# The layer norm's factor and offset of the token tiles, on GpSimd at the head of a sublayer or on VectorE among its later steps

## The chip, the cores and the metric

The kernel runs on one core of a Trainium2 chip. The metric is the time of one launch in microseconds (us) of the device. The engines are named as in the profile: PE is TensorE (PEld its weight loads), DVE is VectorE, ACT is ScalarE, POOL is GpSimd, SP is SyncE, whose queue issues nearly all loads.

## What is computed

Two networks of the same plan run behind each other in fp32 on 256 tokens of 1024 channels: six sublayers in all. Each takes the residual stream, modulates it, runs a mixer or an expert layer, and normalizes the weighted sum:

```python
for i in range(DEPTH):
    ...
    hx = modulate(xs, sh1, sc1)                  # h * (1 + scale) + shift
    ...                                          # a mixer gives yx
    xs = layer_norm(alpha * xs + g1 * yx, ln_g[i, 0], ln_b[i, 0])
    hx = modulate(xs, sh2, sc2)
    ...                                          # peer, or a second mixer, gives fx
    xs = layer_norm(alpha * xs + g2 * fx, ln_g[i, 1], ln_b[i, 1])
```

The layer norm ends in `(h - mu) * rsqrt(var + eps) * g + b`, where g and b are rows of 1024 numbers. The sublayers s = 0 to 5 are mixer_ab, peer, mixer_pool, peer, moba and gdn. peer is an expert layer: queries, scores against keys, two rounds of top 16, a gather of experts by one-hot products, and sums.

## The kernel before

**Tiles.** The stream of tokens is two tiles `xs[0]` and `xs[1]` of 128 tokens by 1024 channels. Every product in fp32 is three matmuls (`mm3`, L130 to L132) of operands that are split into a rounded part and a rest. For a weight tile of 128x1024 `split_w` makes the rounded part on ACT (L94) and the rest on DVE (L95, both inputs in SBUF). For activations `split_a` does the same in pieces of up to 512 columns (L124 on ACT, L125 on DVE). A weight comes by a 512 KB load into one of four `raw` buffers (SP queue, L87), and its two parts go into one of three buffers each.

**Head of a sublayer.** `restart(s)`, for s = 1 to 5, stands between the norm of the sublayer before and the first product. The norm leaves `xs` normalized, but without g and b (L322 and L324 the reciprocal root, L368 a column, L373 on ACT and L375 on DVE the tiles). PE transposes `xs` (L409), and ACT (L413) and DVE (L415, from PSUM) put g, b and the modulation into one affine step, which gives `hf`; `split_a` makes the pair `h` from it, and the first products of the sublayer read `h` piece by piece. The residual needs `xs` with g and b too, but not before the sublayer's end, where `mix` (L346 to L348) adds the result. For it GpSimd multiplies `xs` by the row of g and adds the row of b, from the tile `lngb` that is loaded in the head:

```python
self.tail = i0.ins, i1.ins
for t in range(NT):
    x = self.xs[t]
    nc.gpsimd.tensor_tensor(x, x, gb[:, 0], op=ALU.mult)      # L424
    nc.gpsimd.tensor_tensor(x, x, gb[:, 1], op=ALU.add)       # L425
```

These are four operations of 128x1024 in each head, twenty in all.

**What sets the order.** The framework's scheduler orders each engine's instructions by the dependences and its own model of time. `issue_after(i)` keeps an instruction behind i, and `keep_in_program_order` keeps the code's order. `tail` is the pair of the last affine steps of the head, and `held` makes the splits of the two weights behind the first one wait for `tail`.

**What follows the heads.** In peer (s = 1 and 3) 16 steps `hp` each make a query by a linear step of 24 matmuls of 256 columns, then scores (L756) and two top-16 searches on DVE (L964 to L968); in steps 4 and 5 `xs` is also kept in DRAM (L771) for the residual. mixer_pool (s = 2) starts with two halves `nb` of four steps with 512-column products, moba (s = 4) with four halves, between which `ada_cols` multiplies and sums tiles of a modulation matrix on DVE (L284). gdn (s = 5) begins with a loop over b of linear steps and convolutions, and a small product with `wab` for its gates (split on DVE in L1156).

**The end.** The last norm has g and b in it: `mix_end` gives ACT and GpSimd the columns from 704 (tile 0) or 832 (tile 1) on (L380 to L382), and DVE the columns before them (L385, L386). L387 stores the result.

Of the kernel before, what the change touches and what calls it, by code (L numbers as in the profile page):

```python
# [11 lines left out]
F32 = mybir.dt.float32  # L12
# [10 lines left out]
NT = 2  # L23
# [18 lines left out]
class Net:  # L42
    def __init__(self, ctx, tc, a):
# [73 lines left out]
    def split_a(self, pool, src, n, tag, x1=None, x2=None):  # L117
        nc = self.nc
        if x1 is None:
            x1 = pool.tile([P, n], F32R, tag=tag + "1", name=self.nm(tag))  # L120
            x2 = pool.tile([P, n], F32R, tag=tag + "2", name=self.nm(tag))
        for o in range(0, n, 512):
            s = slice(o, min(o + 512, n))
            nc.scalar.activation(x1[:, s], src[:, s], AF.Copy)  # L124
            nc.vector.tensor_tensor(x2[:, s], src[:, s], x1[:, s].bitcast(F32), op=ALU.subtract)  # L125
        return x1, x2
# [147 lines left out]
    def ada_cols(self, i, cb, row):  # L274
# [86 lines left out]
    def mix_end(self, t):  # L361
# [9 lines left out]
        if self.last is None:  # L371
# [5 lines left out]
        g, b = self.last[:, 0], self.last[:, 1]  # L377
        k = (704, 832)[t]
        c = slice(k, D)
        nc.scalar.activation(z[:, c], z[:, c], AF.Identity, bias=nmr, scale=r)  # L380
        nc.gpsimd.tensor_tensor(z[:, c], z[:, c], g[:, c], op=ALU.mult)
        nc.gpsimd.tensor_tensor(z[:, c], z[:, c], b[:, c], op=ALU.add)  # L382
        c = slice(0, k)
        self.tc.keep_in_program_order(
            nc.vector.scalar_tensor_tensor(z[:, c], z[:, c], mv[:, 0:1], g[:, c], op0=ALU.subtract, op1=ALU.mult))  # L385
        nc.vector.scalar_tensor_tensor(z[:, c], z[:, c], r, b[:, c], op0=ALU.mult, op1=ALU.add)  # L386
        nc.sync.dma_start(self.a["out"][t], z)  # L387
# [6 lines left out]
    def restart(self, s, pool, h=None):  # L394
# [16 lines left out]
        for q, pt in enumerate(pts):  # L411
            kc = q * 2
            i0 = nc.scalar.activation(hf[:, kc], pt[:, 0].rearrange("p t c -> p (t c)"), AF.Identity,  # L413
                                 bias=ab[:, 1, kc:kc + 1], scale=ab[:, 0, kc:kc + 1])
            i1 = nc.vector.tensor_scalar(hf[:, kc + 1], pt[:, 1].rearrange("p t c -> p (t c)"),  # L415
                                    ab[:, 0, kc + 1:kc + 2], ab[:, 1, kc + 1:kc + 2], op0=ALU.mult, op1=ALU.add)
            for k in ((kc, kc + 1), (kc + 1, kc + 2)) if q == 0 else ((kc, kc + 2),):
                k = slice(*k)
                self.split_a(None, *(z[:, k].rearrange("p k t -> p (k t)") for z in (hf,)), (k.stop - k.start) * T, "",
                             *(z[:, k].rearrange("p k t -> p (k t)") for z in h))  # L420
        self.tail = i0.ins, i1.ins
        for t in range(NT):
# [291 lines left out]
    def peer(self, li, s, pool):  # L714
# [28 lines left out]
        with tc.tile_pool(name=self.nm("tk"), bufs=1) as tk:  # L743
# [19 lines left out]
            for hp in range(16):  # L763
# [224 lines left out]
    def mixer_pool(self, h, pool):  # L988
# [38 lines left out]
    def moba(self, h, pool):  # L1027
# [98 lines left out]
    def gdn(self, h, hf, pool):  # L1126
# [537 lines left out]
```

## Time and profile before

| what | value |
|---|---|
| time, median of 3 runs | 2500.62 us (2500.24 to 2500.70) |
| the profiled execution, its own time | 2504.04 us |
| its span, first to last instruction | 2502.2 us |
| mean granted clock of PE | 0.986 of full |
| PE busy | 2410.9 us (96%) |
| DVE busy | 1864.3 us (75%) |
| ACT busy | 1195.4 us (48%) |
| POOL busy | 158.5 us (6%) |
| DMA | 210 GB/s over the span |

All times within the program are of the profiled execution, whose own time stands beside its span: 1.8 us lie around the span. A row of the timeline gives the start, the duration, the engine, the line, the operation and its operands, and in brackets how long the engine was idle before it and what released it. `x2` at the end of a timeline row means that two alike are merged, with their time together.

### The profile page before, as it was taken

The numbers are of one execution on the slowest core, as the hardware profiler recorded it, in microseconds if no ns is written. First come the engines' busy times: TensorE is split into PE (matmuls) and PEld (weight loads), VectorE is DVE, ScalarE is ACT, GpSimd is POOL, SyncE is SP. The second block draws the span as 40 slices with busy tenths as digits, with TensorE's granted clock in tenths as the row PEclk, the third lists the DMA queues.
The fourth block names the chain that finished last, engine by engine and source line by source line (L and its number), as shares of the span: only waits on it lengthen the run. The fifth ranks groups of instructions, "written<-read, shape, count | busy, mean of one in ns | idle before, by whom it ended". The sixth has DMA issues, their size and how long they took to land.

```text
span 2502.2 us, 41876 instructions
## 1 busy us (share of the span) xinstructions
PE 2410.9 (96%) x15572; PEld 2131.3 (85%) x15572; DVE 1864.3 (75%) x3825; ACT 1195.4 (48%) x1980; POOL 158.5 (6%) x126
## 2 busy tenths in 40 slices
PE   8999899999999999998999999999999998998997
PEld 5875799999998777887899999998778887897886
DVE  3446699767776788876699767776888767787866
ACT  3345444544445444454544544445444554446533
POOL 1111200000000000001100000000000001003431
PEclk9999999999999999999999999999999999998999
DMA  8436557765557888975456765557899876863312
GB/s 296 132 134 228 179 169 220 238 194 177 176 173 245 290 306 307 311 246 185 160 171 216 239 200 177 172 179 241 302 310 311 271 219 198 278 221 121 110 59 68
DMA packets 196557, 527.42 MB, mean 211 GB/s; under 512 B 22104, under 2 KB 84984, under 8 KB 195200
## 3 DMA queue, kind: packets, MB, share of 16 engines
q1 hardware_dynamic: 160128, 488.70, 60.2%
q10 hardware_dynamic: 36224, 36.04, 4.1%
q8 instruction: 122, 2.00, 0.3%
q14 instruction: 83, 0.68, 0.1%
HBM read 489.76 MB, written 34.90 MB: 210 GB/s over the span
## 4 chain that ended last, share of the span: by engine, by line
PE 65%; DVE 14%; DMA 4%; issue 3%; ACT 2%; POOL 1%; SPq 0%; POOLq 0%; DVEq 0%; ACTq 0%
PE mm L132 10%; PE mm L131 10%; PE mm L130 10%; PE acc L132 9%; PE acc L130 9%; PE acc L131 9%; PE acc L827 4%; DVE w L95 4%; DMA raw<-peer_v 2%; ACT w L94 1%; DVE tk L965 1%; PE mm L1345 1%; DVE h L125 1%; DVE idx L968 1%; DVE raw L284 1%
## 5 line engine op out<-in xcount | busy, mean ns | idle before, releaser
L94 ACT ACTIVATE w<-raw 128x1024 fp32r<-128x1024 f32 x686 | 725.5, 1058 | 942.2 <-PE mm L131 490.1
L95 DVE TENSOR_TENSOR w<-raw,w 128x1024 fp32r<-128x1024 f32 x686 | 847.7, 1237 | 352.2 <-ACT w L94 350.6
L130 PE MATMUL mm<-h,w 128*128 128x256 f32 x2624 | 762.0, 291 | 4.4 <-ACT w L94 2.5
L131 PE MATMUL mm<-h,w 128*128 128x256 f32 x2624 | 747.8, 285 | 13.1 <-DVE h L125 13.0
L132 PE MATMUL mm<-h,w 128*128 128x256 f32 x2624 | 749.8, 286 | 7.0 <-DVE w L95 6.8
L131 PEld LDWEIGHTS mm<-h,w 128*128 128x128 f32 x2624 | 507.2, 193 | 16.5 <-DVE h L125 15.4
L132 PEld LDWEIGHTS mm<-h,w 128*128 128x128 f32 x2624 | 506.2, 193 | 11.2 <-DVE w L95 11.0
L130 PEld LDWEIGHTS mm<-h,w 128*128 128x128 f32 x2624 | 507.4, 193 | 6.4 <-ACT w L94 2.9
L130 PE MATMUL acc<-w,x 128*128 128x512 f32 x1024 | 405.2, 396 | 2.3 <-ACT x L124 2.2
L132 PE MATMUL acc<-w,x 128*128 128x512 f32 x1024 | 402.6, 397 | 4.2 <-DVE x L125 4.0
L131 PE MATMUL acc<-w,x 128*128 128x512 f32 x1024 | 404.1, 395 | 0.0
L132 PEld LDWEIGHTS acc<-w,x 128*128 128x128 f32 x1024 | 192.2, 188 | 58.1 <-DVE x L125 13.4
L130 PEld LDWEIGHTS acc<-w,x 128*128 128x128 f32 x1024 | 192.7, 188 | 49.6 <-ACT x L124 5.4
L131 PEld LDWEIGHTS acc<-w,x 128*128 128x128 f32 x1024 | 192.5, 188 | 44.5
L816 DVE TENSOR_TENSOR hot<-cols,sel 128x512 f32<-128x512 f32 x128 | 88.6, 692 | 112.6 <-PE acc L827 112.6
L324 POOL TENSOR_TENSOR rs<-rv,mhalf 128x1 f32<-128x1 f32 (+2 forms) x38 | 31.8, 836 | 2152.8 <-DVE rv L322 2151.7
L124 ACT ACTIVATE x<-ga 128x256 fp32r<-128x256 f32 x256 | 104.3, 408 | 110.9 <-DVE ga L862 105.1
L820 DVE TENSOR_SCALAR hot<-cols,sel 128x128 f32<-128x128 f32 x512 | 142.2, 341 | 0.0
L827 PE MATMUL acc<-hot 128*128 128x128 f32 x1024 | 134.9, 274 | 0.0
L827 PEld LDWEIGHTS acc<-hot 128*128 128x128 f32 x1024 | 125.4, 192 | 0.0
L132 PE MATMUL acc<-w,h 128*128 128x512 f32 (+1 forms) x296 | 116.4, 395 | 8.5 <-DVE h L125 8.5
L130 PE MATMUL acc<-w,h 128*128 128x512 f32 (+1 forms) x296 | 116.9, 398 | 4.4 <-ACT h L124 4.3
(381 smaller groups left out, 2747.2 us busy)
## 6 DMA issues: line engine op xcount, KB each, us to landing
raw<-peer_u SPq DMA_DIRECT2D x256, 512.0 KB, 3.6
raw<-peer_v SPq DMA_DIRECT2D x256, 512.0 KB, 4.7
raw<-adaT SPq DMA_DIRECT2D x96, 512.0 KB, 4.5
spill<-ga ACTq DMA_DIRECT2D x242, 128.0 KB, 2.3
ga<-spill SPq DMA_DIRECT2D x242, 128.0 KB, 4.5
raw<-ada SPq DMA_DIRECT2D x48, 512.0 KB, 3.9
raw<-ab_w_in SPq DMA_DIRECT2D x32, 512.0 KB, 3.6
raw<-peer_wq SPq DMA_DIRECT2D x32, 512.0 KB, 3.5
```

What stands on the lines that cost most here:

```text
L94: nc.scalar.activation(w1, raw, AF.Copy)
L95: nc.vector.tensor_tensor(w2, raw, w1.bitcast(F32), op=ALU.subtract)
L124: nc.scalar.activation(x1[:, s], src[:, s], AF.Copy)
L125: nc.vector.tensor_tensor(x2[:, s], src[:, s], x1[:, s].bitcast(F32), op=ALU.subtract)
L130: mm(ps, l[0], r[0], start=start, stop=False)
L131: mm(ps, l[0], r[1], start=False, stop=False)
L132: mm(ps, l[1], r[0], start=False, stop=stop)
L284: nc.vector.scalar_tensor_tensor(rx, rx, 1.0, cb[x], op0=ALU.mult, op1=ALU.mult, accum_out=part[:, x, k:k + 1])
L324: nc.gpsimd.tensor_tensor(r, v, self.mhalf[:, :n], op=ALU.pow)
L816: nc.vector.tensor_tensor(hot[:, 0], iota[:, None].to_broadcast([P, G, P]), sel[:, 0, n0:n0 + G, None].to_broadcast([P, G, P]), op=ALU.is_ ...
L820: nc.vector.tensor_scalar(hot[:, 1, g], iota, sel[:, 1, n:n + 1], sel[:, 2, n:n + 1], op0=ALU.is_equal, op1=ALU.mult)
L827: nc.tensor.matmul(ps[:, g * P:(g + 1) * P], hot[:, 0, g], hot[:, 1, g], start=True, stop=True)
```

## The change

The operations L424 and L425 leave GpSimd. `restart` puts them on a list `todo`, and `later()` takes one of it and issues it on DVE behind `tail`. It is called once in each step `hp` from 2 on of peer, in each step of mixer_pool's second half, in each even step of moba's first two halves, and in each round b from 1 on of gdn's convolution loop; `mix_begin`, at the end of a sublayer, does what is left. With it go:

- `tail` is now the pair of the last split of `h`, so that the held weights and `ada_cols` (L284, now L287) stand behind it.
- peer keeps `xs` in DRAM in steps 6 and 7.
- The last norm is done by DVE alone, over all 1024 columns (L384, L385).
- A tile `X` of gdn has a place of its own in SBUF, where it shared one with `lngb`.

```diff
+        self.ends = i.ins, j.ins                      # split_a: its last pair
...
+                with self.tc.issue_after(self.tail[1]):
+                    nc.vector.scalar_tensor_tensor(rx, rx, 1.0, cb[x], op0=ALU.mult, op1=ALU.mult, accum_out=part[:, x, k:k + 1])
...
+        while self.todo:
+            self.later()
...
-        nc.gpsimd.tensor_tensor(z[:, c], z[:, c], g[:, c], op=ALU.mult)
-        nc.gpsimd.tensor_tensor(z[:, c], z[:, c], b[:, c], op=ALU.add)
...
+            nc.vector.scalar_tensor_tensor(z, z, mv[:, 0:1], g, op0=ALU.subtract, op1=ALU.mult))
+        nc.vector.scalar_tensor_tensor(z, z, r, b, op0=ALU.mult, op1=ALU.add)
...
-        self.tail = i0.ins, i1.ins
-        for t in range(NT):
-            x = self.xs[t]
-            nc.gpsimd.tensor_tensor(x, x, gb[:, 0], op=ALU.mult)
-            nc.gpsimd.tensor_tensor(x, x, gb[:, 1], op=ALU.add)
+        self.tail = self.ends
+        self.todo = [(self.xs[t], gb[:, x], (ALU.mult, ALU.add)[x]) for t in range(NT) for x in range(2)]
...
+    def later(self):
+        if self.todo:
+            x, y, op = self.todo.pop(0)
+            with self.tc.issue_after(self.tail[1]):
+                self.nc.vector.tensor_tensor(x, x, y, op=op)
...
-                if hp in (4, 5):
-                    tc.keep_in_program_order(nc.scalar.dma_start(kept[hp - 4], self.xs[hp - 4]))
+                if hp > 1:
+                    self.later()
+                if hp in (6, 7):
+                    tc.keep_in_program_order(nc.scalar.dma_start(kept[hp - 6], self.xs[hp - 6]))
...
-        X, XT = (pt_([P, NT * D], tg).rearrange("p (t h c) -> p t h c", t=NT, h=H) for tg in ("b1", "XT"))
+        X, XT = (pt_([P, NT * D], tg).rearrange("p (t h c) -> p t h c", t=NT, h=H) for tg in ("X", "XT"))
```

GpSimd has 24 instructions fewer (the twenty and four of the end), DVE 19 more, ACT 4 fewer. PE has as many as before, and on SP one load (the last norm's rows) stands 23 places earlier.

DVE, head of s = 1 (peer), from the first splits of `h` to the first top-16 search, before (a row's `out<-in` are the program's names with numbers; `w` is a weight's rest, `vals` a search):

```order
L125 TENSOR_TENSOR h_2376<-hf_2384,h_2375 128x256 x2
L415 TENSOR_SCALAR hf_2384<-mm_2389,ab_2380 128x256
L125 TENSOR_TENSOR h_2376<-hf_2384,h_2375 128x512
L415 TENSOR_SCALAR hf_2384<-mm_2390,ab_2380 128x256
L125 TENSOR_TENSOR h_2376<-hf_2384,h_2375 128x512
L95 TENSOR_TENSOR w_2463<-raw_2460,w_2462 128x1024
L125 TENSOR_TENSOR h_2376<-hf_2384,h_2375 128x512
L95 TENSOR_TENSOR w_2496<-raw_2493,w_2495 128x1024
L95 TENSOR_TENSOR w_2529<-raw_2526,w_2528 128x1024
L95 TENSOR_TENSOR w_2572<-raw_2569,w_2571 128x1024
L964 MAX vals_2455<-sc_2459 128x8
```

The same place after:

```order
L126 TENSOR_TENSOR h_2376<-hf_2384,h_2375 128x256 x2
L414 TENSOR_SCALAR hf_2384<-mm_2389,ab_2380 128x256
L126 TENSOR_TENSOR h_2376<-hf_2384,h_2375 128x512
L414 TENSOR_SCALAR hf_2384<-mm_2390,ab_2380 128x256
L126 TENSOR_TENSOR h_2376<-hf_2384,h_2375 128x512 x2
L429 TENSOR_TENSOR xs_96<-xs_96,lngb_2385 128x1024
L96 TENSOR_TENSOR w_2459<-raw_2456,w_2458 128x1024
L96 TENSOR_TENSOR w_2492<-raw_2489,w_2491 128x1024
L96 TENSOR_TENSOR w_2525<-raw_2522,w_2524 128x1024
L969 MAX vals_2451<-sc_2455 128x8
L969 MAX vals_2452<-sc_2455 128x8
```

The last split of `h` moved ahead of the weight's split, the first of the four moved operations (L429) stands between them, and the first search has three weight splits ahead of it where it had four; the other three L429 follow among the searches.

DVE, head of s = 4 (moba), from the norm's end on, before:

```order
L368 SCALAR_TENSOR_TENSOR nmr_22102<-mv_22096,rs_22100 128x1
L375 TENSOR_SCALAR xs_22038<-xs_22038,mv_22096,rs_22100 128x512
L284 SCALAR_TENSOR_TENSOR raw_22272,adap_22271<-raw_22272,cb_22238 128x512 x2
L415 TENSOR_SCALAR hf_22118<-mm_22123,ab_22112 128x256
L415 TENSOR_SCALAR hf_22118<-mm_22121,ab_22112 128x256
L415 TENSOR_SCALAR hf_22118<-mm_22122,ab_22112 128x256
L125 TENSOR_TENSOR h_22117<-hf_22118,h_22116 128x256 x2
```

The same place after:

```order
L380 TENSOR_SCALAR xs_22038<-xs_22038,mv_22096,rs_22100 128x512
L414 TENSOR_SCALAR hf_22118<-mm_22123,ab_22112 128x256
L414 TENSOR_SCALAR hf_22118<-mm_22124,ab_22112 128x256
L414 TENSOR_SCALAR hf_22118<-mm_22121,ab_22112 128x256
L414 TENSOR_SCALAR hf_22118<-mm_22122,ab_22112 128x256
L126 TENSOR_TENSOR h_22117<-hf_22118,h_22116 128x256
```

The two L284, which stood between the norm and the first affine step, have left this place; they come behind the head's splits.

DVE, the end of the program, before:

```order
L368 SCALAR_TENSOR_TENSOR nmr_26012<-mv_25970,rs_25974 128x1
L385 SCALAR_TENSOR_TENSOR xs_22037<-xs_22037,mv_25970,b_25808 128x704
L386 SCALAR_TENSOR_TENSOR xs_22037<-xs_22037,rs_25974,b_25808 128x704
L368 SCALAR_TENSOR_TENSOR nmr_26020<-mv_26006,rs_26010 128x1
L385 SCALAR_TENSOR_TENSOR xs_22038<-xs_22038,mv_26006,b_25808 128x832
L386 SCALAR_TENSOR_TENSOR xs_22038<-xs_22038,rs_26010,b_25808 128x832
```

After, the same six stand there with 1024 columns each in L384 and L385, and neither ACT nor GpSimd has a part in these tiles.

## Rows read from the trace of the kernel before

**Rows 1.** The page: busy time of the engines; shares of the chain

```profile
PE 2410.9 (96%) x15572; PEld 2131.3 (85%) x15572; DVE 1864.3 (75%) x3825; ACT 1195.4 (48%) x1980; POOL 158.5 (6%) x126
...
PE 65%; DVE 14%; DMA 4%; issue 3%; ACT 2%; POOL 1%; SPq 0%; POOLq 0%; DVEq 0%; ACTq 0%
```

**Rows 2.** Groups by line, GpSimd: shapes xcount | busy, mean ns | idle before

```profile
L425 POOL TENSOR_TENSOR xs<-xs,lngb 128x1024 f32<-128x1024 f32 x10 | 27.9, 2799 | 0.3
```

**Rows 3.** Timeline of the head of s = 1: DVE, GpSimd, then PE

```profile
293.04 0.53 DVE L415 TENSOR_SCALAR hf<-mm,ab 128x256 f32<-128x256 f32 x1
293.50 2.40 DVE L125 TENSOR_TENSOR h<-hf,h 128x512 fp32r<-128x512 f32 x1
...
298.60 3.38 DVE L95 TENSOR_TENSOR w<-raw,w 128x1024 fp32r<-128x1024 f32 x1
...
304.67 1.21 DVE L95 TENSOR_TENSOR w<-raw,w 128x1024 fp32r<-128x1024 f32 x1
...
311.23 0.48 DVE L964 MAX8 vals<-sc 128x8 f32<-128x128 f32 x2
...
292.68 5.45 POOL L424 TENSOR_TENSOR xs<-xs,lngb 128x1024 f32<-128x1024 f32 x2 [3.40 <-ACT h L124]
...
304.80 0.58 PE L131 MATMUL mm<-h,w 128*128 128x256 f32 x1 [1.33 <-DVE h L125]
...
308.91 0.61 PE L756 MATMUL mm<-keys,qT 128*128 128x128 f32 x4
```

**Rows 4.** Windows: length, busy (x) of PE PEld DVE ACT POOL, PEclk, DMA share, GB/s

```profile
350.00:430.00 80.00, 76.55 (x620) 74.66 (x619) 79.93 (x248) 37.46 (x60) 0.00 (x0) 1.00 0.67 195
...
1173.00:1178.00 5.00, 5.00 (x13) 3.81 (x13) 4.25 (x5) 1.06 (x1) 0.00 (x0) 0.50 0.32 110
1178.00:1225.00 47.00, 47.00 (x243) 40.68 (x242) 23.83 (x26) 26.85 (x38) 0.00 (x0) 1.00 0.61 203
...
2137.00:2175.00 38.00, 34.05 (x188) 29.11 (x187) 26.31 (x51) 14.79 (x18) 0.00 (x0) 0.96 0.83 288
...
2262.00:2275.00 13.00, 9.05 (x45) 7.28 (x46) 8.37 (x6) 1.79 (x3) 10.32 (x9) 0.54 0.34 117
2275.00:2315.00 40.00, 40.00 (x337) 37.21 (x336) 32.23 (x73) 35.14 (x83) 5.90 (x7) 1.00 0.37 119
```

**Rows 5.** Timeline of the head of s = 2: DVE, then PE

```profile
1165.15 8.69 DVE L125 TENSOR_TENSOR h<-hf,h 128x256 fp32r<-128x256 f32 x5
...
1172.70 0.79 PE L132 MATMUL acc<-w,h 128*128 128x512 f32 x1 [4.07 <-DVE h L125]
```

**Rows 6.** Timeline of the head of s = 3: DVE

```profile
1237.75 3.23 DVE L125 TENSOR_TENSOR h<-hf,h 128x256 fp32r<-128x256 f32 x2
...
1247.59 0.68 DVE L125 TENSOR_TENSOR h<-hf,h 128x512 fp32r<-128x512 f32 x1
```

**Rows 7.** Timeline of the head of s = 4: DVE, then PE

```profile
2100.87 2.29 DVE L368 SCALAR_TENSOR_TENSOR nmr<-mv,rs 128x1 f32<-128x1 f32 x1 [0.66 <-POOL rs L324]
...
2103.54 2.85 DVE L284 SCALAR_TENSOR_TENSOR raw<-raw,cb 128x512 f32<-128x512 f32 x1
...
2103.67 1.97 PE L409 MATMUL mm<-ident,xs 128*128 128x128 f32 x8 [3.27 <-DVE xs L375]
```

**Rows 8.** Timeline of the head of s = 5: DVE, then GpSimd

```profile
2258.46 1.74 DVE L95 TENSOR_TENSOR w<-raw,w 128x1024 fp32r<-128x1024 f32 x1 [1.63 <-ACT w L94]
...
2266.19 2.42 DVE L1156 TENSOR_TENSOR wab<-wab,wab 128x128 fp32r<-128x128 f32 x1
...
2256.75 5.65 POOL L424 TENSOR_TENSOR xs<-xs,lngb 128x1024 f32<-128x1024 f32 x2 [5.88 <-DMA lngb<-ln_rows]
```

**Rows 9.** Timeline of the program's end: DVE, then GpSimd

```profile
2491.51 0.95 DVE L385 SCALAR_TENSOR_TENSOR xs<-xs,mv,b 128x704 f32<-128x704 f32 x1
...
2494.10 1.07 DVE L385 SCALAR_TENSOR_TENSOR xs<-xs,mv,b 128x832 f32<-128x832 f32 x1
...
2497.30 0.59 POOL L382 TENSOR_TENSOR xs<-xs,b 128x192 f32<-128x192 f32 x1
```

More of the change, by code (lines that the diff above doesn't have):

```diff
@@ L68, in __init__ @@
         self.held = 0
+        self.todo = []
     def nm(self, s):
@@ L123, in split_a @@
             s = slice(o, min(o + 512, n))
-            nc.scalar.activation(x1[:, s], src[:, s], AF.Copy)
-            nc.vector.tensor_tensor(x2[:, s], src[:, s], x1[:, s].bitcast(F32), op=ALU.subtract)
+            i = nc.scalar.activation(x1[:, s], src[:, s], AF.Copy)
+            j = nc.vector.tensor_tensor(x2[:, s], src[:, s], x1[:, s].bitcast(F32), op=ALU.subtract)
+        self.ends = i.ins, j.ins
         return x1, x2
@@ L283, in ada_cols @@
                 rx = r[:, x * 512:(x + 1) * 512]
-                nc.vector.scalar_tensor_tensor(rx, rx, 1.0, cb[x], op0=ALU.mult, op1=ALU.mult, accum_out=part[:, x, k:k + 1])
+                with self.tc.issue_after(self.tail[1]):
+                    nc.vector.scalar_tensor_tensor(rx, rx, 1.0, cb[x], op0=ALU.mult, op1=ALU.mult, accum_out=part[:, x, k:k + 1])
             if k == KC - 1:
@@ L377, in mix_end @@
         g, b = self.last[:, 0], self.last[:, 1]
-        k = (704, 832)[t]
-        c = slice(k, D)
-        nc.scalar.activation(z[:, c], z[:, c], AF.Identity, bias=nmr, scale=r)
-        nc.gpsimd.tensor_tensor(z[:, c], z[:, c], g[:, c], op=ALU.mult)
-        nc.gpsimd.tensor_tensor(z[:, c], z[:, c], b[:, c], op=ALU.add)
-        c = slice(0, k)
         self.tc.keep_in_program_order(
-            nc.vector.scalar_tensor_tensor(z[:, c], z[:, c], mv[:, 0:1], g[:, c], op0=ALU.subtract, op1=ALU.mult))
-        nc.vector.scalar_tensor_tensor(z[:, c], z[:, c], r, b[:, c], op0=ALU.mult, op1=ALU.add)
+            nc.vector.scalar_tensor_tensor(z, z, mv[:, 0:1], g, op0=ALU.subtract, op1=ALU.mult))
+        nc.vector.scalar_tensor_tensor(z, z, r, b, op0=ALU.mult, op1=ALU.add)
         nc.sync.dma_start(self.a["out"][t], z)
@@ L412, in restart @@
             kc = q * 2
-            i0 = nc.scalar.activation(hf[:, kc], pt[:, 0].rearrange("p t c -> p (t c)"), AF.Identity,
+            nc.scalar.activation(hf[:, kc], pt[:, 0].rearrange("p t c -> p (t c)"), AF.Identity,
                                  bias=ab[:, 1, kc:kc + 1], scale=ab[:, 0, kc:kc + 1])
-            i1 = nc.vector.tensor_scalar(hf[:, kc + 1], pt[:, 1].rearrange("p t c -> p (t c)"),
+            nc.vector.tensor_scalar(hf[:, kc + 1], pt[:, 1].rearrange("p t c -> p (t c)"),
                                     ab[:, 0, kc + 1:kc + 2], ab[:, 1, kc + 1:kc + 2], op0=ALU.mult, op1=ALU.add)
@@ L995, in mixer_pool @@
         for nb in range(2):
-            for t, ps in enumerate(self.lin_nat(a["pool_w_in"][nb], 4, xa)):
+            pss = [self.acc() for _ in xa]
+            for _ in self.lin_steps(a["pool_w_in"][nb], 4, xa, pss):
+                if nb == 1:
+                    self.later()
+            for t, ps in enumerate(pss):
                 nc.scalar.copy(hin[:, t, nb * 512:nb * 512 + 512], ps)
@@ L1039, in moba @@
                     next(ada, None)
+                else:
+                    self.later()
             for t, ps in enumerate(pss):
@@ L1475, in gdn @@
             conv_mm(b)
+            if b:
+                self.later()
             next(ga, None)
```

## The prediction

> **What bounds the kernel now.** I read the page first. TensorE is busy for 96% of the span and has 65% of the chain that ended last; VectorE, busy for 75%, has another 14%, and GpSimd is busy for only 6% [rows 1]. So the bulk of the time is products, and the work that the change moves is small: GpSimd's additions (L425) take 27.9 us for ten and its multiplications about as much [rows 2], with nobody reading their result before the sublayer's end. By their own duration they cost nothing. The question is what else they do, and for that I read the timeline of each head, VectorE against GpSimd.
>
> There a pattern shows. In the head of s = 1 GpSimd's first pair starts at 292.68 and lasts 5.45 us, and the second pair (mean 2.80 us each [rows 2]) follows, so GpSimd works until about 304. In this stretch VectorE's split of 128x512 takes 2.40 us and its weight split 3.38 us; the next weight split, at 304.67, takes 1.21 us [rows 3]. In s = 3 the head's last split of 128x512 takes 0.68 us, where the first two of 128x256, as many columns together, take 3.23 [rows 6]. The affine step L415, whose input is in PSUM, takes 0.53 us in the middle of the slow stretch [rows 3]. So it is VectorE's operations with two inputs in SBUF that stretch to 2.4 to 3.5 times while GpSimd works on `xs`. TensorE waits for them (1.33 us before 304.80 [rows 3] is one of several such waits), and behind these waits its granted clock falls: 0.50 in the 5 us from 1173, 0.54 in the 13 us from 2262, where it is 1.00 in the long stretches behind [rows 4]. That is the lower of its two levels, 1.2 GHz against 2.4.
>
> The Trainium skill, page "SBUF — State Buffer", section "Who interferes with whom", has a rule for it: a VectorE instruction with two inputs in SBUF contends with a GpSimd instruction that reads SBUF, since its second input comes through the port that GpSimd uses; with one such input it does not. The rows agree (2.40 against 0.68 us, and 0.53 for the step from PSUM). By it the whole excess goes once GpSimd's reads are gone.
>
> **The change part by part.** I walk through each head with VectorE's durations from outside GpSimd's work: 0.68 us for 512 columns of split, 1.21 us for a weight split, 0.53 us for L415. The moved operation, 128x1024 with two inputs in SBUF, isn't in the trace on VectorE; the weight split has the same shape and operands, so I take 1.21 us for it. Twenty of them are 24.2 us of new VectorE work.
>
> *s = 1 (peer).* From 293.50 on three splits and one L415 stand ahead of the end of `h`: 3 x 0.68 + 0.53 gives 296.1, and I allow 0.6 us for ACT's rounded parts, which must come first (an estimate): 296.7, against 304.67. Then come the first L429 and the weight split that the second query waits for, to 299.1, and 22 matmuls at 0.123 us (76.55 us for 620 [rows 4]), to 301.8. Before, this point was 308.91 [rows 3]: TensorE is 7.1 us earlier. But VectorE, which does the top-16 searches from here on, is busy for 79.93 of the 80 us from 350, and TensorE already loses 3.45 us there [rows 4]. Its first search could start at 302.5 instead of 311.23, 8.7 us earlier, with three L429 and one weight split more behind it than before: 4.8 us of that are paid back, 3.9 stay. So the gain lies between 3.9 and 7.1; I take 4.7, near VectorE's end, as VectorE is the fuller of the two. If TensorE's clock falls in its new wait before 299.1, 22 matmuls take 2 to 3 us longer, and 2 is left.
>
> *s = 2 (mixer_pool).* Five splits, 2048 columns, take 8.69 us from 1165.15 [rows 5]; at 0.68 for 512 they take 2.7, so `h` ends 5.9 us earlier. TensorE's wait of 4.07 us for it [rows 5] goes with that, and so should the 5.0 us at clock 0.50 behind it, worth up to 2.5 more; I take 1.3 of it, since the weight splits follow close. 7.2, from 6 to 8.4. The four L429 fall in the second half, where VectorE is busy for 23.83 of 47 us [rows 4]: covered. Without that cover they would cost 4.8.
>
> *s = 3 (peer).* From 1237.75 to the last split's end at 1248.27 VectorE does 2048 columns of split, two L415 and one weight split [rows 6]: 10.5 us for 2.7 + 1.1 + 1.2 = 5.0. So 5.5 on TensorE's line; on VectorE's, three L429 (3.6) go off: 1.9. I take 3.2, from 1.5 to 5.5.
>
> *s = 4 (moba).* Two L284 of 2.85 us stand between the norm and the first L415, and L368, a single column, takes 2.29 us [rows 7]. The L284 go behind the head's splits, and L368 shrinks to that of a column: I count 2.0. TensorE's transposes, 1.97 us, ran beside the L284 [rows 7] and now stand on the path. 5.7 - 2.0 + 2.0 gives 5.7, and some 0.5 more comes from the splits that overlap GpSimd's end: 6.2 for the first products. What limits this gain stands behind it: from 2137 to 2175 the DMA engines are 83% busy at 288 GB/s, and TensorE is idle for 4 of 38 us [rows 4]. The loads start earlier only as buffers come free earlier. I take 4.2, from 1 to 6.2.
>
> *s = 5 (gdn).* The four operations from 2258.46 to 2268.61 (two weight splits, the last split of `h`, and L1156 of 128 columns) take 10.15 us [rows 8], for 1.2 + 0.7 + 1.2 + 0.3 = 3.4: 6.7. From 2262 on TensorE is busy for 9.05 us at clock 0.54 [rows 4]; at full clock this is 4.2 less. The first L429 stands ahead of a weight split that TensorE waits for, 1.2 back. 9.7, from 5.5 (no gain of clock) to 10.8. The other three L429 find VectorE busy for 32.23 of 40 us from 2275 [rows 4], 7.8 us free for 3.6. One wait is new: L429 needs `lngb`, for which GpSimd waited 5.88 us up to 2256.75 [rows 8]; VectorE gets there later than that, at about 2259, so it costs nothing, but a load later by more than 2 us would hold the weight splits queued behind it.
>
> *The end.* Now VectorE alone: L385 takes 0.95 us for 704 columns and 1.07 for 832 [rows 9], so about 1.25 for 1024, and four in a row from 2491.51 end at 2496.7 with their gaps. GpSimd's last piece ended at 2497.89 [rows 9]. 1.2 gained, from 0.8 to 1.6.
>
> The rest costs nothing: peer's keeping of `xs` in DRAM two steps later is hidden, since it is read only at the sublayer's end; the load of the last norm's rows 23 places earlier in SP's queue is 1 MB among many.
>
> Sum: 4.7 + 7.2 + 3.2 + 4.2 + 9.7 + 1.2 = 30.2 us. The profiled execution took 2504.04 us with a span of 2502.2, so 2473.8 on its scale; it lies 3.4 us over the median of 2500.62, on whose scale it is 2470.4. The low ends give 2 + 6 + 1.5 + 1 + 5.5 + 0.8 = 16.8, so 2483.8, and the high ones 7.1 + 8.4 + 5.5 + 6.2 + 10.8 + 1.6 = 39.6, so 2461.0.
>
> **The rivals.**
>
> *A, the forecast:* 2470, between 2464 and 2477 by the usual spread of its terms.
>
> *B, the whole gain is kept:* TensorE's lead survives the searches and the loads, and the clock comes back everywhere: 2461 to 2464. For it: behind the searches TensorE is the fuller engine again. Against it: VectorE's 79.93 of 80 us.
>
> *C, the later bound takes the gain of three heads back:* in s = 1 and 3 VectorE is the bound and pays for its four L429 with all that it won, and in s = 4 the loads set the pace anyway. What is left is 7.2 + 9.7 + 1.2 = 18.1, so 2482.5; 2477 to 2484 with part of it. For it: the same row, and 288 GB/s. Against it: the excess that goes from VectorE in these heads (8.0 us at the end of `h` in s = 1) is larger than the 4.8 us that come back. The Trainium skill, page "Perfetto Trace Analysis", section "Optimizing Scalar/DVE Operations", speaks for this case: where VectorE is saturated, giving work to another engine, even GpSimd, may make sense. It adds that the two share a port, so that this might not help; the slow splits above agree with the addition, and no run here shows which weighs more.
>
> *D, slower:* VectorE's splits are slow in the heads for another reason (TensorE's and ACT's writes, say) and stay at 2.4 us without GpSimd. Then nothing is won there, and the L429 are paid where VectorE is full: eight in peer (9.7) and one in gdn's head (1.2), so 2511.5. It decides if a split of 512 columns still takes over 2 us in the head. Against it: the weight split falls from 3.38 to 1.21 us just where GpSimd ends in s = 1, and the last split of s = 3 is back at 0.68.
>
> *E, the change does little:* the scheduler's order puts other waits in the heads that eat what goes, within 5 us of 2500.6. The order shows `h` closed earlier on VectorE in each head, which speaks against it.
>
> **How the numbers follow.** A 0.54, B 0.14, C 0.26, D 0.03, E 0.03. The forecast is A's, 2470. The range 2461 to 2484 takes in A, B and C with the ends of the unknown terms; outside lie D, E and the outer parts of B and C. About 0.2% (5 us) is what a measurement of this kernel can tell from no change; faster by more is A, B and C, 0.94, within it E, 0.03, slower D, 0.03.
>
> **What would show it right or wrong.** Splits of 128x512 in all five heads at about 0.7 us and no weight split over 1.3 there; L429 at about 1.2 us. The first scores of s = 1 some 7 us nearer to the head's start, and the last product of its top-16 stretch 4 to 5 us earlier: if it is 7, B is right, if it is under 2, C. PEclk at 1.00 where it was 0.50 behind the heads of s = 2 and 5; if it still falls there, these terms lose up to 5 us together. In s = 4 TensorE's idle time from 2137 on should grow by the part that the loads keep. Wrong altogether would be splits at 2.4 us without GpSimd, or a head in which VectorE stands still before L429 for `lngb`.

## The result, and the profile after

The changed kernel takes 2460.77 us (median of 4 runs, 2458.49 to 2464.38) against 2500.66 us, a ratio of 0.9842 with a 95% interval of 0.9825 to 0.9859. That is 39.9 us less, where 30.2 were forecast: at the very low end of the range (2461; 0.2 us beyond it, which is within the spread of the runs), 9 us under the predicted 2470. The profiled execution took 2461.12 us, with a span of 2459.3 us.

The page after, the lines that answer to [rows 1]: busy time of the engines, then the shares of the chain that ended last.

```profile
PE 2394.7 (97%) x15572; PEld 2119.9 (86%) x15572; DVE 1852.0 (75%) x3845; ACT 1192.7 (48%) x1977; POOL 101.6 (4%) x102
...
PE 72%; DVE 15%; DMA 6%; ACT 3%; issue 3%; POOL 1%; ACTq 0%; SPq 0%; DVEq 0%; POOLq 0%
```

VectorE got 20 more instructions and is busy for 12 us less. The groups by line show why. First the kernel before (line, engine, operation, shapes, count | busy us, mean ns of one | idle before):

```profile
L95 DVE TENSOR_TENSOR w<-raw,w 128x1024 fp32r<-128x1024 f32 x686 | 847.7, 1237 | 352.2 <-ACT w L94 350.6
...
L284 DVE SCALAR_TENSOR_TENSOR raw<-raw,cb 128x512 f32<-128x512 f32 x48 | 35.6, 774 | 7.6 <-DMA raw<-adaT 7.6
L125 DVE TENSOR_TENSOR h<-hf,h 128x512 fp32r<-128x512 f32 x15 | 23.4, 1571 | 0.0
...
L125 DVE TENSOR_TENSOR h<-hf,h 128x256 fp32r<-128x256 f32 x10 | 11.0, 1136 | 0.0
...
L368 DVE SCALAR_TENSOR_TENSOR nmr<-mv,rs 128x1 f32<-128x1 f32 x12 | 4.7, 390 | 4.6 <-POOL rs L324 4.4
...
L1156 DVE TENSOR_TENSOR wab<-wab,wab 128x128 fp32r<-128x128 f32 x1 | 2.4, 2422 | 0.0
```

and the same groups, with the moved operations (L429), in the changed kernel:

```profile
L96 DVE TENSOR_TENSOR w<-raw,w 128x1024 fp32r<-128x1024 f32 x686 | 843.0, 1231 | 335.1 <-ACT w L95 333.4
...
L287 DVE SCALAR_TENSOR_TENSOR raw<-raw,cb 128x512 f32<-128x512 f32 x48 | 31.2, 685 | 2.6 <-DMA raw<-adaT 2.5
L429 DVE TENSOR_TENSOR xs<-xs,lngb 128x1024 f32<-128x1024 f32 x20 | 24.2, 1215 | 0.0
...
L126 DVE TENSOR_TENSOR h<-hf,h 128x512 fp32r<-128x512 f32 x15 | 10.2, 689 | 0.4 <-ACT h L125 0.2
...
L126 DVE TENSOR_TENSOR h<-hf,h 128x256 fp32r<-128x256 f32 x10 | 3.9, 417 | 0.0
L373 DVE SCALAR_TENSOR_TENSOR nmr<-mv,rs 128x1 f32<-128x1 f32 x12 | 1.9, 158 | 5.1 <-POOL rs L327 4.8
L1167 DVE TENSOR_TENSOR wab<-wab,wab 128x128 fp32r<-128x128 f32 x1 | 0.3, 292 | 0.0
```

The six groups that stretched are 34 us shorter (13.2 and 7.1 us in the splits of `h`, 4.7 in the weight splits, 4.4 in L284, 2.8 in L368, 2.1 in `wab`); the twenty L429 take 24.2 us. So VectorE's sum hardly changes. What changes is where it is spent: the 34 us stood in the heads, ahead of TensorE, and the 24 stand among later steps.

The head of s = 1, which answers to [rows 3]; timeline of VectorE, then of TensorE (start us, duration us, engine, line, operation):

```profile
290.98 0.69 DVE L126 TENSOR_TENSOR h<-hf,h 128x512 fp32r<-128x512 f32 x1
...
292.04 1.48 DVE L126 TENSOR_TENSOR h<-hf,h 128x512 fp32r<-128x512 f32 x2
293.43 1.22 DVE L429 TENSOR_TENSOR xs<-xs,lngb 128x1024 f32<-128x1024 f32 x1
294.57 3.49 DVE L96 TENSOR_TENSOR w<-raw,w 128x1024 fp32r<-128x1024 f32 x3
297.97 0.48 DVE L969 MAX8 vals<-sc 128x8 f32<-128x128 f32 x2
...
295.00 0.71 PE L759 MATMUL mm<-keys,qT 128*128 128x128 f32 x4 [0.33 <-ACT qT L768]
```

`h` is closed 2.5 us after the 512-column splits begin, where it took 11.2, and TensorE waits for nothing longer than 0.34 us here. The windows that answer to [rows 4] (length, busy us and counts of PE, PEld, DVE, ACT, POOL, then PEclk, DMA share, GB/s) show the clock: it stays at the upper level behind the heads of s = 2 and s = 5, where it was 0.50 and 0.54.

```profile
1160.00:1165.00 5.00, 4.91 (x21) 4.05 (x22) 5.00 (x6) 1.73 (x2) 0.00 (x0) 1.00 0.73 269
...
2222.00:2234.00 12.00, 11.47 (x93) 9.96 (x92) 9.91 (x17) 8.89 (x17) 4.46 (x7) 1.00 0.47 162
2234.00:2247.00 13.00, 13.00 (x110) 12.84 (x109) 11.98 (x25) 9.73 (x15) 0.00 (x0) 1.00 0.60 209
```

The prediction read the clock behind these two heads alone. Before, it was at the lower level behind those of s = 1 and s = 3 too, where the changed kernel has 1.00:

```profile
297.70:307.90 10.20, 6.39 (x26) 5.81 (x27) 8.93 (x5) 1.58 (x3) 6.50 (x3) 0.50 0.25 72
...
1243.20:1250.00 6.80, 5.28 (x23) 4.99 (x24) 6.20 (x6) 1.58 (x2) 2.78 (x1) 0.50 0.16 40
```

From the first head to the last stage the windows at 0.50 make 54.5 us before (from 297.7, 1171.5, 1243.2, 2103.4, 2161.4, 2260.4, 2335.5 and 2383.2 on) and 17.0 us after (from 358.4, 1290.2 and 2293.7 on). Their sums, before and after:

```profile
sum 54.50, PE 41.66 PEld 37.36 DVE 45.95 ACT 15.22 POOL 31.14; mean PE 5.21 PEld 4.67 DVE 5.74 ACT 1.90 POOL 3.89
...
sum 17.00, PE 14.83 PEld 14.34 DVE 15.47 ACT 6.61 POOL 3.32; mean PE 4.94 PEld 4.78 DVE 5.16 ACT 2.20 POOL 1.11
```

If TensorE's busy time in these windows were half as long at 1.00, the difference is some 13 of the 40 us (an estimate from these sums; 13 as well with r1_after). So about a third of the gain is clock that came back.

To tell where the 40 us are, I cut each profiled execution at the row of VectorE that starts a head: the column `nmr` of token tile 1 (L368 before, L373 after), and at the end that of tile 0. These are single executions; where the changed kernel was profiled a second time (r1_after, below), its stages lay within 1.3 us of the first.

| stage, us | before | after | gain | forecast |
|---|---|---|---|---|
| start to head of s = 1 | 289.3 | 286.8 | 2.5 | 0 |
| s = 1, peer | 872.3 | 865.8 | 6.5 | 4.7 |
| s = 2, mixer_pool | 73.1 | 66.0 | 7.2 | 7.2 |
| s = 3, peer | 866.2 | 861.2 | 5.0 | 3.2 |
| s = 4, moba | 150.0 | 142.7 | 7.3 | 4.2 |
| s = 5, gdn | 240.5 | 228.0 | 12.6 | 9.7 |
| the end | 10.8 | 8.9 | 1.9 | 1.2 |

The first row isn't the change's: the lead of 2.6 us is there at 30 us, where both kernels do the same, and the granted clock from 21.2 to 28.0 us was 0.50 in the execution of before and 1.00 in that of after. It is most of the 3.4 us by which the profiled execution of before lay over its median. The other six make 40.4 us, against 39.9 by the medians.

### The profile page after: what moved, and what is told of

Read it like the earlier page. It is cut to its first block, busy times and chain, and to the rows that moved or that the text cites. A ratio compares the mean times of both kernels' runs of the same rounds, so it can differ in the third digit from the quotient of the medians.

```text
span 2459.3 us, 41846 instructions
## 1 busy us (share of the span) xinstructions
PE 2394.7 (97%) x15572; PEld 2119.9 (86%) x15572; DVE 1852.0 (75%) x3845; ACT 1192.7 (48%) x1977; POOL 101.6 (4%) x102
## 4 chain that ended last, share of the span: by engine, by line
PE 72%; DVE 15%; DMA 6%; ACT 3%; issue 3%; POOL 1%; ACTq 0%; SPq 0%; DVEq 0%; POOLq 0%
PE mm L134 11%; PE mm L133 11%; PE mm L132 11%; PE acc L134 10%; PE acc L133 10%; PE acc L132 10%; PE acc L832 5%; DVE w L96 4%; DMA raw<-peer_v 3%; ACT w L95 2%; DVE tk L970 1%; PE mm L1356 1%; DVE idx L973 1%; DVE raw L287 1%; DVE idx L972 1%
## 5 line engine op out<-in xcount | busy, mean ns | idle before, releaser
L133 PE MATMUL mm<-h,w 128*128 128x256 f32 x2624 | 745.6, 284 | 1.2 <-DVE h L126 1.0
L134 PEld LDWEIGHTS mm<-h,w 128*128 128x128 f32 x2624 | 504.3, 192 | 10.8 <-DVE w L96 10.4
L133 PEld LDWEIGHTS mm<-h,w 128*128 128x128 f32 x2624 | 505.3, 193 | 3.7 <-DVE h L126 2.5
L133 PE MATMUL acc<-w,x 128*128 128x512 f32 x1024 | 404.2, 395 | 0.0
L133 PEld LDWEIGHTS acc<-w,x 128*128 128x128 f32 x1024 | 192.6, 188 | 44.4
L133 PE MATMUL acc<-w,h 128*128 128x512 f32 (+1 forms) x296 | 115.2, 390 | 3.0 <-DVE w L96 3.0
```

Of the source, the lines that this page charges most:

```text
L133: mm(ps, l[0], r[1], start=False, stop=False)
L134: mm(ps, l[1], r[0], start=False, stop=stop)
```

## The experiments

All edits are against the changed kernel. Three questions: is it GpSimd that stretches VectorE in the heads, and what of its work; what the place in the order is worth, and what the engine; and what the twenty operations cost where they now are.

**GpSimd back in the heads, the new order kept (e1_gpsimd_head).**

```diff
-        self.todo = [(self.xs[t], gb[:, x], (ALU.mult, ALU.add)[x]) for t in range(NT) for x in range(2)]
+        for t in range(NT):
+            x = self.xs[t]
+            nc.gpsimd.tensor_tensor(x, x, gb[:, 0], op=ALU.mult)
+            nc.gpsimd.tensor_tensor(x, x, gb[:, 1], op=ALU.add)
```

> The changed kernel with one part undone: the factor and offset are again four GpSimd operations in each head; the later tail, the later products of the modulation matrix, the last norm on VectorE and gdn's own tile stay. Theory (GpSimd's operations stretch VectorE's two-input operations): about 2494 us, that is the changed kernel's 2461 plus the 34 us by which the stretched groups of rows are longer in the trace of the kernel before; the splits of h at 1.5 us or more again. Rival (the gain came from the new order, the tail and the products moved out of the head): below 2475 us.

Measured: 2496.03 us (2492.62 to 2498.49), beside 2500.39 for the kernel before on the same chip, a ratio of 0.9979 (0.9969 to 0.9989). Timeline of s = 1's head, VectorE, then GpSimd:

```profile
292.15 2.40 DVE L126 TENSOR_TENSOR h<-hf,h 128x512 fp32r<-128x512 f32 x1
...
294.93 5.17 DVE L126 TENSOR_TENSOR h<-hf,h 128x512 fp32r<-128x512 f32 x2
300.03 4.52 DVE L96 TENSOR_TENSOR w<-raw,w 128x1024 fp32r<-128x1024 f32 x2
...
291.58 5.20 POOL L423 TENSOR_TENSOR xs<-xs,lngb 128x1024 f32<-128x1024 f32 x2 [3.64 <-DVE h L126]
296.75 5.58 POOL L424 TENSOR_TENSOR xs<-xs,lngb 128x1024 f32<-128x1024 f32 x2
```

The splits are slow again, and the stages s = 1 to 4 take 872.3, 74.9, 866.4 and 149.0 us, as before the change to within 1.8. So in these the later tail and the later products of the modulation matrix bring nothing while GpSimd stays. Only gdn keeps a part, 234.2 us for 240.5: there the scheduler sets another order, in which TensorE reaches the gates' products 4 us earlier, and the windows at 0.50 make 10.2 us in the stage, where they made 23.9. Whether the later tail or the tile `X` of its own brings that order was not parted. The rival falls, but for these 6 us.

**GpSimd writes, but doesn't read (e2_memset_head).**

```diff
-        self.todo = [(self.xs[t], gb[:, x], (ALU.mult, ALU.add)[x]) for t in range(NT) for x in range(2)]
+        for t in range(NT):
+            for _ in range(6):
+                nc.gpsimd.memset(self.xs[t], 1.0)
```

> The same, but GpSimd writes only: six memsets of 128x1024 for each token tile stand in the head in place of the four operations, so the factor and offset, and with them the residual, are left out. Theory (it is GpSimd's reading of SBUF that stretches VectorE): splits of 128x512 at 0.7 us while the memsets run, and 2452 to 2462 us. Rival (any work of GpSimd on SBUF, or its writes, do it): splits of 1.5 us or more beside the memsets, and over 2480 us.

Measured: 2459.00 us (2457.68 to 2461.30). VectorE, then GpSimd, in s = 1's head:

```profile
292.23 0.69 DVE L126 TENSOR_TENSOR h<-hf,h 128x512 fp32r<-128x512 f32 x1
...
293.29 1.47 DVE L126 TENSOR_TENSOR h<-hf,h 128x512 fp32r<-128x512 f32 x2
...
290.32 9.91 POOL L423 MEMSET xs<- 128x1024 f32 x11 [0.30 <-PE mm L408]
```

GpSimd is as busy beside the splits as it was in e1, for 10 us, and they take 0.69 us each. So neither that GpSimd is busy nor that it writes SBUF stretches VectorE. What the memsets lack is the reading of two inputs; that it is the reading, and not the arithmetic that goes with it, fits all rows, but no run parts the two.

**The twenty operations left out (e3_left_out, then r2_left_out beside r1_after).**

```diff
-        self.todo = [(self.xs[t], gb[:, x], (ALU.mult, ALU.add)[x]) for t in range(NT) for x in range(2)]
+        self.todo = []
```

> The changed kernel without the twenty operations at all (factor and offset of the residual left out), so it shows what they cost on VectorE. Theory (the moved operations are covered, as the gain of each head was kept): 2456 to 2461 us. Rival, the prediction's own charge (paid where VectorE is full: 3.6 us in each peer, 1.2 in gdn): 2450 to 2453 us.

> The changed kernel itself, unaltered, beside the next two on one chip, because single executions of these kernels lie up to 6 us apart and the differences in question are smaller. Expected: 2459 to 2463 us.

> The changed kernel without the twenty operations, as in e3_left_out, beside the changed kernel. By the stages of single profiles the twenty cost 7.6 us, by the medians 2.3. Theory (mostly covered): 2 to 4 us under r1_after. Rival (paid where VectorE is full, as the prediction charged): 7 to 9 us under it.

Measured: 2458.45 us (2455.50 to 2461.27) at first, and in a second comparison 2459.66 (2455.96 to 2462.68) beside 2463.18 (2461.67 to 2468.22) for the changed kernel. So the 24.2 us on VectorE cost 2 to 4 us of time, though the intervals of single runs overlap. By stages of the two pairs of profiles, s = 1 pays 3.1 and 1.7 us, s = 3 1.7 and 1.1, gdn 1.9 and 1.4; the others go both ways, by up to 1.7 us. In these three stages that is 6.7 and 4.2 us, and the prediction had charged 5.9 there (2.4, 2.3 and 1.2): not far off, and far under the 24.2 us that the operations last.

**Later, but still on GpSimd (e4_gpsimd_later).** The load of the rows goes behind later weights, so that GpSimd can't start earlier.

```diff
-        self.tc.keep_in_program_order(nc.sync.dma_start(gb, self.a["ln_rows"][s - 1:s].to_broadcast([P, 2, D])))
+        self.rows = gb, self.a["ln_rows"][s - 1:s].to_broadcast([P, 2, D])
...
+            if self.rows is not None:
+                self.tc.keep_in_program_order(self.nc.sync.dma_start(*self.rows))
+                self.rows = None
...
-                self.nc.vector.tensor_tensor(x, x, y, op=op)
+                self.nc.gpsimd.tensor_tensor(x, x, y, op=op)
```

> The twenty operations stay on GpSimd, but run later: the load of their rows is issued among the sublayer's later steps, so they start behind the head. It parts the place from the engine. If only the place matters: 2455 to 2463 us, like the changed kernel or better, since VectorE has less to do. If GpSimd's reading costs wherever VectorE works on two inputs: some 11 us of GpSimd in each sublayer, in which weight splits of 1.2 us become up to 3.4; VectorE has slack for part of it in mixer_pool, moba and gdn and none in the two peers, so 3 to 8 us more in each peer and 2465 to 2480 us in all.

Measured: 2490.28 us (2486.66 to 2493.54), slower than both expectations. The delay worked in two heads only: in s = 3 to 5 the load landed in time all the same, GpSimd ran beside the splits of `h`, and the stages (868.7, 147.0, 236.5 us) lie between 2.5 us above and 4 us under those before. In s = 1 and s = 2 it ran later, beside weight splits alone; VectorE, then GpSimd, in each:

```profile
294.93 11.27 DVE L96 TENSOR_TENSOR w<-raw,w 128x1024 fp32r<-128x1024 f32 x4 [0.26 <-ACT w L95]
...
294.95 13.52 POOL L432 TENSOR_TENSOR xs<-xs,lngb 128x1024 f32<-128x1024 f32 x4 [7.03 <-ACT w L95]
...
1170.30 14.38 DVE L96 TENSOR_TENSOR w<-raw,w 128x1024 fp32r<-128x1024 f32 x5 [1.49 <-ACT w L95]
...
1170.02 12.45 POOL L432 TENSOR_TENSOR xs<-xs,lngb 128x1024 f32<-128x1024 f32 x4 [13.66 <-DMA lngb<-ln_rows]
```

Weight splits of 1.2 us take 2.8 and 2.9 us there on the mean. These two stages (868.4 and 69.1 us) win 3.8 and 4.0 us of the 6.5 and 7.2, and the rest is lost to the same contention in another place. It is a mixed run, but in the two heads where it did what it should, the place alone brings a little over half.

**On VectorE, but in the head (e8_vector_head).** As e1_gpsimd_head, with `nc.vector` in place of `nc.gpsimd`.

> The twenty operations on VectorE, but in the head, where the scheduler puts the first ahead of the first affine step and the others around the last split of h. It parts the engine from the place. Theory (the place costs what stands ahead of h's last split, 1 to 2.4 us a head, and in gdn the wait for the load of the rows, which landed 5.9 us after GpSimd was ready): 2466 to 2476 us. Rival (VectorE has room in the head as well): 2458 to 2464 us.

Measured: 2478.79 us (2477.37 to 2480.40): beyond the expected 2476, and 22 of the 40 us are kept. Not all of the 22 are the engine's, since the rest of the change stands here as in e1. From e1 to e8 (2496.03 to 2478.79), where only the engine differs, it is 17 us; from e8 to the changed kernel, where only the place differs, 18; and e1 itself was 4 us faster than the kernel before. The largest part of the 18 is gdn, 236.0 us for 228.0, and the row shows why; timeline of VectorE at its head:

```profile
2232.50 0.64 DVE L380 TENSOR_SCALAR xs<-xs,mv,rs 128x512 f32<-128x512 f32 x1
2237.58 1.23 DVE L423 TENSOR_TENSOR xs<-xs,lngb 128x1024 f32<-128x1024 f32 x1 [4.44 <-DMA lngb<-ln_rows]
2238.72 0.54 DVE L414 TENSOR_SCALAR hf<-mm,ab 128x256 f32<-128x256 f32 x1
```

VectorE stands still for 4.44 us, for rows that nobody needs yet, with the affine step of the next product queued behind. In the other heads the cost is 0.5 to 2.9 us a stage.

**The old order without GpSimd (e7_old_order).** The tail is the last affine steps again, and `ada_cols` isn't held behind it.

```diff
-        self.tail = self.ends
+        self.tail = i0.ins, i1.ins
...
-                with self.tc.issue_after(self.tail[1]):
-                    nc.vector.scalar_tensor_tensor(rx, rx, 1.0, cb[x], op0=ALU.mult, op1=ALU.mult, accum_out=part[:, x, k:k + 1])
+                nc.vector.scalar_tensor_tensor(rx, rx, 1.0, cb[x], op0=ALU.mult, op1=ALU.mult, accum_out=part[:, x, k:k + 1])
```

> The changed kernel with the tail at the last affine steps again and the products of the modulation matrix free to stand in moba's head; GpSimd stays out of the heads. It shows what the new order alone is worth. Theory (the order is worth little once GpSimd is out: the two products cost 0.7 us each beside PE's transposes): 2459 to 2465 us, moba's stage at most 1.5 us longer than the changed kernel's 142.7. Rival (the order matters in moba, where the products stood ahead of the first affine step): moba's stage 145 us or more.

Measured: 2467.80 us, but from 2461.93 to 2472.49, so the size is open, from 1 to 12 us. moba's stage is 143.3 us, 0.6 longer, so the two products in its head cost little without GpSimd, as expected. What I had not expected is the others; the profiled execution is the longest of the four, and in it s = 1 and s = 3 are 1.7 and 1.9 us longer and gdn 5.1. With the old tail an L429 (here L428) may stand ahead of the last split of `h`; VectorE in s = 1:

```profile
294.04 1.22 DVE L428 TENSOR_TENSOR xs<-xs,lngb 128x1024 f32<-128x1024 f32 x1
295.18 0.68 DVE L126 TENSOR_TENSOR h<-hf,h 128x512 fp32r<-128x512 f32 x1
```

which puts `h` off by 1.1 us. The new tail forbids that.

**The last norm shared again (e5_end_shared).** `mix_end` with the columns from 704 and 832 on for ACT and GpSimd, as before.

> The changed kernel with one part undone: the last norm is again shared by VectorE, ACT and GpSimd. From the last column of the norm to the end of the span it takes 8.9 us in the changed kernel and 10.7 in the one before. Theory (GpSimd's pieces end last and stretch VectorE's): 10.5 to 10.9 us there and 2461 to 2465 us in all. Rival (the shorter end came from elsewhere, such as the earlier load of the last norm's rows): 9 us there.

Measured: 2462.63 us (2462.20 to 2468.28), and 10.1 us from the last `nmr` of tile 0 to the end of the span, for 8.9 and 10.8. So 1.2 of the 1.9 us come from the shared norm, a little less than expected. The other 0.7 lies behind the last operation: from there to the end of the span it is 4.4 us before, 3.7 here and in the changed kernel, but 4.1 in e1, which has the changed kernel's norm. So it can't be given to the change.

**gdn's own GpSimd products on VectorE (e9_gdn_vector, then r3_gdn_vector).**

```diff
-                G_.tensor_tensor(lo, LT[hq][:, t], lmask[:, lv, None].to_broadcast([P, 4, P]), op=ALU.mult)
+                V_.tensor_tensor(lo, LT[hq][:, t], lmask[:, lv, None].to_broadcast([P, 4, P]), op=ALU.mult)
...
-                G_.tensor_tensor(dr[:, t], dT[:, t, hs], rk[:, t, :, None].to_broadcast([P, 2, 64]), op=ALU.mult)
+                V_.tensor_tensor(dr[:, t], dT[:, t, hs], rk[:, t, :, None].to_broadcast([P, 2, 64]), op=ALU.mult)
...
-            G_.tensor_tensor(xr, xr, dr, op=ALU.mult)
+            V_.tensor_tensor(xr, xr, dr, op=ALU.mult)
```

> The changed kernel with gdn's own GpSimd products (the masked copies lo, 24 of 128x512, and those of dr and xr) on VectorE as well, to see if the rule carries to a place where VectorE is fuller: 85% busy from 2287 to 2325 of the changed kernel's profile, GpSimd 10 of each 13 to 25 us. Theory (GpSimd's reading stretches VectorE's two-input operations there too, and TensorE waits for those): 2452 to 2459 us. Rival (24 times 0.69 us more on VectorE lengthen the chain of the inversion as much as they free): 2460 to 2470 us.

> gdn's GpSimd products on VectorE, as in e9_gdn_vector, beside the changed kernel. If the 3.1 us that gdn's stage was shorter in one profile are real: 2 to 4 us under r1_after. Rival (the order of that profile, no gain): within 1.5 us of it.

Measured: 2460.78 us (2460.02 to 2461.56), then 2462.88 (2458.60 to 2463.57) beside 2463.18: no difference. gdn's stage is shorter in both profiles (224.8 and 224.5 us for 228.0 and 229.1), and its windows at 0.50 make 3.4 us for 10.2, so 2.4 and 3 of these 3.1 and 4.6 us can be clock (half of TensorE's busy time that is no longer at 0.50). But mixer_pool's is longer by 2.4 and 2.5 us (68.4 and 68.9 for 66.0 and 66.3) and moba's by 1.0 and 1.5, though nothing is changed there and in mixer_pool VectorE's instructions stand in the same order. In mixer_pool's last 11 us the granted clock is 0.84 where it is 1.00 in the changed kernel. It falls behind a wait of TensorE for a weight split, 1.93 and 2.45 us (PE L133 at 1213.13 and 1213.25) for 0.88 in the changed kernel, and the split itself starts 1.0 and 1.6 us later in the stage; why it does is open. So gdn's stage gains, and the kernel doesn't.

## Why the prediction was right, and where it was off

**The mechanism** stood as the prediction put it. Splits of `h` at 0.69 us, weight splits at 1.2, `wab` at 0.29; e1 shows that GpSimd's four operations stretched them, and e2 that as long a work of memsets doesn't. What stretches is no factor of 2.4 to 3.5, as the prediction read it, but a wait (last section): the single column went from 0.16 to 2.29 us. Rivals D (slow for another reason) and E (the change does little) are out, and C too: behind the searches of s = 1 TensorE still leads by 8 us (below). The Trainium skill's rule, page "SBUF — State Buffer", section "Who interferes with whom", says that the contention needs a GpSimd instruction that reads SBUF and not one that only writes it: e2 agrees, at 0.69 us beside 10 us of memsets. The other rule that was weighed, page "Perfetto Trace Analysis", section "Optimizing Scalar/DVE Operations", on giving work of a saturated VectorE to another engine, did not hold in the peers, whose searches keep VectorE at 100%: with the four operations in the same place, VectorE's stages (e8) are 6.0 and 2.5 us shorter than GpSimd's (e1). The page itself warns of the shared port.

**The sizes** were too small in all heads but one. By the sum, 39.9 us against high ends of 39.6, what happened is rival B, the whole gain kept, which had a chance of 0.14. That the sums agree so closely is partly luck: s = 1 to 3 stayed under their high ends (18.7 for 21.0) and s = 4, s = 5 and the end went over theirs (21.8 for 18.6). Step by step:

- *s = 1, 4.7 for 6.5, and s = 3, 3.2 for 5.0.* The step that failed is the start. I let the scores of the first query come behind the second query's products, as they did before; in the changed order they stand ahead of them (PE L759 at 295.00). So the first search starts 10.7 us earlier as seen from the head (311.23 against 297.97, less the 2.5 us of the start), not 8.7. TensorE's own lead behind the head is 8.5 us, not 7.1, by the scores of the second query:

```profile
312.23 0.61 PE L756 MATMUL mm<-keys,qT 128*128 128x128 f32 x4
...
301.21 0.61 PE L759 MATMUL mm<-keys,qT 128*128 128x128 f32 x4
```

`h` is closed 0.7 us earlier than counted, and TensorE's wait before the second query's weight split, on which the low end of 2 rested, did not come: the scores fill it. The charge behind the start was right. The last search, before and after:

```profile
365.65 0.27 DVE L966 MAX8 vals<-tk 128x8 f32<-128x128 f32 x1
...
357.35 0.28 DVE L971 MAX8 vals<-tk 128x8 f32<-128x128 f32 x1
```

It starts 5.8 us earlier as seen from the head, so 4.9 of the 10.7 are paid back on VectorE, where 4.8 were charged. TensorE leads by 8.2 us at the last scores (346.16 against 356.84), waits 1.75 us for a weight split right behind the searches (357.48), where the clock falls for 3.4 us, and keeps 6.5. So the gain does lie between VectorE's line and TensorE's, nearer to VectorE's, as forecast; both lines lay higher, at 5.8 and 8.5 for 3.9 and 7.1. s = 3 is the same: 3.8 and 6.5 for 1.9 and 5.5.

- *s = 2, 7.2 for 7.2.* The clock's share was taken right: 1.00 where it was 0.50.
- *s = 4, 4.2 for 7.3.* The first half of the step was right: the first 512-column halves come 6.2 us earlier (ACT's copy of 2121.53 at 2094.18, a lead of 27.4 where it was 21.1 at the head). What failed is that the loads would take 2 of it back. ACT's waits for moba's weights, before:

```profile
ACT w L94 <- DMA raw<-moba_qk: 12.3, 5, 5.6
...
ACT w L94 <- DMA raw<-moba_vz: 8.7, 4, 3.9
```

and after (us in total, times, longest):

```profile
ACT w L95 <- DMA raw<-moba_vz: 12.3, 7, 3.0
ACT w L95 <- DMA raw<-moba_qk: 9.5, 5, 3.6
```

21.0 and 21.8 us: the stretch that is bound by loads has not grown; it begins earlier as a whole. The loads follow the buffers, which the faster head frees earlier, so this load-bound stretch moved with its head. The clock had a part that no term held: before, it was 0.50 for 3.4 us from 2103.4 and from 2161.4, with TensorE busy for 6.5 of the 6.8; after, it is 1.00 in the whole stage.

- *s = 5, 9.7 for 12.6*, over its high end of 10.8. By the gates' first operation on VectorE the lead had grown by 11.8 us (25.3 us behind the head for 13.5). The charge of 1.2 us for the first L429 was wrong, since TensorE did not wait for the weight split behind it, and with the clock at 1.00 for 71 us behind the head, the gates' products and those around them lost nothing. Further on the clock falls in both kernels, for 10.2 us before and 10.2 after, at other places. e1 shows that a part of the 12.6 is the order and not GpSimd: with GpSimd in the head the new order still kept 6.3 us of gdn's stage. I had costed the later tail and the tile `X` at nothing; e7, with the old tail, is 5.1 us longer there in one profile.
- *The end, 1.2 for 1.9.* VectorE's part was right: its last operation ends 5.2 us behind the last `nmr` of tile 0, where GpSimd's ended 6.4 behind. The other 0.7 us lie between the last operation and the end of the span, and e5 and e1 don't tie them to the change.

What is common to the heads is on TensorE's side: behind each it came out further ahead than the forecast had it (8.5 for 7.1, 6.5 for 5.5, 6.2 kept for 4.2 in moba, 11.8 for 9.7 in gdn): waits that were allowed for didn't come, and the clock stayed up behind heads where I hadn't read its fall. The charge for the moved operations was about right.

## What to carry to other kernels

An operation on an idle engine is not free if one on the path has to take turns with it: look for rows whose duration changes while another engine works, and compare the same shape inside and outside that stretch. Before an operation is put back to an idle engine or a later place, ask who reads its result and when: here the engine was worth 17 us and the place 18, since in the head it either delayed `h` or stood waiting for a load with the path queued behind it. And a busy share of 100% tells that added work costs something, not that it costs its duration: 24 us cost 2 to 4. Count the clock too: a wait of TensorE of 1 to 3 us in a head was followed by up to 14 us at 0.50, so that what went with these waits is more than their length.

## What the hardware showed that I had not expected

Beside GpSimd's operations on `xs`, VectorE's operations with two inputs in SBUF took nearly the same time whatever their size: one column 2.29 us [rows 7], 128 columns 2.42 [rows 8], 512 columns 2.40 and 2.85, 1024 columns 2.8 to 3.4, where GpSimd's own 128x1024 took 2.3 to 3.5. The ends of the operations show why. GpSimd, then VectorE, in the head of s = 1, and GpSimd in those of s = 4 and s = 2, before:

```profile
298.09 2.81 POOL L425 TENSOR_TENSOR xs<-xs,lngb 128x1024 f32<-128x1024 f32 x1
...
300.86 3.34 POOL L425 TENSOR_TENSOR xs<-xs,lngb 128x1024 f32<-128x1024 f32 x1
...
301.90 2.85 DVE L125 TENSOR_TENSOR h<-hf,h 128x512 fp32r<-128x512 f32 x1
...
2100.81 2.34 POOL L424 TENSOR_TENSOR xs<-xs,lngb 128x1024 f32<-128x1024 f32 x1
...
1162.28 2.36 POOL L424 TENSOR_TENSOR xs<-xs,lngb 128x1024 f32<-128x1024 f32 x1 [0.74 <-DMA qg<-pool_q]
```

The split of 512 columns ends at 304.75, 0.55 us behind GpSimd's operation; the weight split of [rows 3] at 301.98, 1.08 behind the one of 298.09; the single column of [rows 7] at 2103.16, 0.01 behind. So it is everywhere: of the 56 two-input operations of VectorE that start while GpSimd works on `xs` in the traces of before, e1 and e4, 55 end at that distance for their size (0.01 us for one column, 0.15 for 128, 0.28 for 256, 0.55 for 512, 1.08 for 1024). The one left started 0.03 us behind GpSimd's and was not stretched. GpSimd's operation takes 2.36 us at 1162.28, with no such operation in its time, 2.81 at 298.09, where the end of a split of 512 columns falls into it, and 3.34 at 300.86, where that of a weight split does. So the two take turns, one whole operation each. What VectorE loses is what is left of GpSimd's operation, up to 2.4 us, so the loss is counted by operations, and a single small column in the wrong place costs as much as a whole tile.
